# Attention by pairs of heads: fp32 values in two halves of TensorE's columns, the maxima's products tied into the order, and the modulations moved to the FFN before

## The chip, the cores and the metric

The kernel runs on one core of a Trainium2 chip. The core has TensorE (PE, matrix products into PSUM, which has eight banks of 128 partitions x 512 fp32), VectorE (DVE), ScalarE (ACT), GpSimd (POOL, which doesn't reach PSUM here) and SyncE (SP, which issues DMAs); each works off its own queue in order. The metric is the device time in microseconds; of the kernel before there are three runs.

## The reference

Two blocks run one after the other on 512 tokens of width 1024, in fp32. The first block mixes three branches (RWKV-7, S5, gated linear attention), then has a cross attention and a convolutional FFN. The second block has two layers, each with modulations of shift, scale and gate from a condition vector; layer 0 is an attention over 256 context and 512 latent tokens, layer 1 an HGRN-2. What the change touches, cut short:

```python
mod_l = silu(c) @ ada_w[i] + ada_b[i]          # 6 vectors of 1024, for latents; the same for the context
q, k = rope(rms_norm(h @ w_q)), rope(rms_norm(h @ w_k));  v = h @ w_v
# 16 heads of 64, 4 key heads: each key head serves 4 query heads
s = einsum('bkgqd,bksd->bkgqs', q, k) * 64 ** -0.5
p = softmax(s, axis=-1)
o = einsum('bkgqs,bksd->bkgqd', p, v)          # latents see all 768 keys, the context its own 256
h = h + gate * (o @ w_o)
```

## The kernel before

Values in fp32 are split into a high and a low part in the type fp32r, and a product is made of three products of parts (`Stream.multiply`, L237, and `tokens`, L250: low times high, high times low, high times high). A product whose operands are plain fp32 is one instruction in the program.

The modulations of layer 0 are made by `Products.steps` (L1483): 12 groups of 512 columns, each with four loads of 512 KB on SP's queue, eight fp32 products of 32 columns (L1494) in four column groups of TensorE (`tile_position`), a copy, and four products that turn the result (L1500). A step is half a group. Four groups are steps of `Context.steps` (L2076), which `conv_ffn` (L1328) takes in as a filler: `b.fill(m % 2)` (L1352) before each pair of feature tiles m from 2 to 21. The other eight groups are steps of `more`, taken inside the attention.

`attn_proj` (L1642) projects tokens to queries, keys and values; it runs while `ahead(0)` already prepares the first pair of heads. The accumulators of the projection are four PSUM banks (`acc2a`), the rest of the work shares four banks (`ps2a`).

`attend` (L1698) does 16 heads. For a pair g, `ahead(g)` is a generator of 13 steps: two with transposes of the queries (each followed by casts on ACT, subtractions on DVE and copies on POOL), then for each of the two heads one step with the scores against the context and four with two products of 384 columns (L1749) whose maxima DVE takes out of PSUM (L1751), and one that turns the maxima and writes their negatives by DMA as a 65th row under the queries. A head has seven units: six key tiles of 128 for the 512 latent queries, and one for the 256 context queries. `scores(h, u)` (L1762) makes two products per tile and ACT's exponential (L1773), then splits the result into `ph` and `pl` on POOL, DVE or ACT by the number of the unit. `values(h, u)` (L1785) makes three products per tile (L1792 to L1794); V has a 65th column of ones, so that a row of the sum is the softmax's denominator. `divide(g)` (L1808) brings the denominators into 12 rows by DMA, inverts them, spreads them by products (L1820) and scales the output.

The loop at L1841 writes the order down: scores of unit i, a step of `ahead` of the next pair, every seventh time a step of the modulations, values of unit i - 3. It is the order of priorities; a planner at compile time, which has times of its own for each instruction, places instructions on each engine's queue by priority and by when it expects their inputs.

Of the kernel before, what the change touches and what calls it, by code (L numbers as in the profile page):

```python
# [17 lines left out]
P = 128  # L18
# [1623 lines left out]
def attn_proj(b, st, hs, t0, tabs, p2, w, Q, K, V):  # L1642
# [5 lines left out]
    def take(i, t, acc):  # L1648
# [49 lines left out]
def attend(b, Q, K2, V, out, high, low, p2, psc, ctx, more):  # L1698
# [5 lines left out]
    Vh, Vl = V  # L1704
# [4 lines left out]
    def ahead(g):  # L1709
# [13 lines left out]
        for c0, c1 in ((0, 2), (2, 6)):  # L1723
            p = psc.tile([P, 512], F32, tag="ps", name="qt")[:, : (c1 - c0) * P]
            for t in range(c0, c1):
                nc.tensor.transpose(p[:, (t - c0) * P : (t - c0 + 1) * P],
                                    Q[kv][:, t, 2 * g % 4 : 2 * g % 4 + 2].rearrange("p h d -> p (h d)"), b.ident)
            s = slice(c0 * P, c1 * P)
            for a in range(2):
# [3 lines left out]
                if g == 0:  # L1733
                    nc.scalar.copy(q2[a][64:, s], q2[a][:64, s].bitcast(F32))
                else:
                    nc.gpsimd.tensor_scalar(q2[a][64:, s], q2[a][:64, s].bitcast(F32), 1.0, 0.0, op0=ALU.mult, op1=ALU.add)
            yield
        mx = p2.tile([P, 2, 6], F32, tag="mx", name="mx")
        m2 = p2.tile([P, 2, 4, 2], F32, tag="m2", name="m2")
        for a in range(2):  # L1740
            sc = psc.tile([P, 2, n0], F32, tag="ps", name="sc")
            for t in range(2):
                nc.tensor.matmul(sc[:, t], q2[a][:, t * P : (t + 1) * P], K2[:, kv, old], start=True, stop=True)
            nc.vector.tensor_reduce(mx[:, a, :2], sc, axis=AX.X, op=ALU.max)
            yield
            for t in range(2, 6):
                for f in range(2):
                    sc = psc.tile([P, 512], F32, tag="ps", name="sc")[:, : T // 2]
                    nc.tensor.matmul(sc, q2[a][:, t * P : (t + 1) * P], K2[:, kv, f * T // 2 : (f + 1) * T // 2],  # L1749
                                     start=True, stop=True)  # L1750
                    nc.vector.tensor_reduce(m2[:, a, t - 2, f : f + 1], sc, axis=AX.X, op=ALU.max)  # L1751
                yield
# [9 lines left out]
    def scores(h, u):  # L1762

        q2, q1 = (q[h % 2] for q in ready[h // 2][:2])
        K1 = ready[h // 2][2]
        kv = h // 4
        p = pss.tile([P, 512], F32, tag="st", name="st")
        for k, q, o in [(u, new, p)] if u < 6 else [(k, old, p[:, k * n0 : (k + 1) * n0]) for k in range(2)]:
            c = slice(k * P, (k + 1) * P)
            nc.tensor.matmul(o, K1[:, c], q1[:, q], start=True, stop=False)  # L1770
            nc.tensor.matmul(o, K2[:, kv, c], q2[:, q], start=False, stop=True)
# [3 lines left out]
        n = 7 * h + u  # L1775
        if n % 5 == 3:
            nc.scalar.copy(ph, pr)  # L1777
        else:
            (nc.vector if n % 5 == 1 else nc.gpsimd).tensor_scalar(ph, pr, 1.0, 0.0, op0=ALU.mult, op1=ALU.add)
        (nc.vector if n % 3 == 1 else nc.gpsimd).tensor_tensor(pl, pr, ph.bitcast(F32), op=ALU.subtract)  # L1780
        return ph, pl

    accs, sums, O, L = {}, {}, {}, {}

    def values(h, u, ph, pl):  # L1785
        kv = h // 4
        if u in (0, 6):
            accs[h] = psa.tile([P, 512], F32, tag="acc", name="acc")[:65, : 4 * P if u == 0 else n0]
        acc = accs[h]
        for k, x in [(u, slice(0, 512))] if u < 6 else [(k, slice(k * n0, (k + 1) * n0)) for k in range(2)]:  # L1790
            first, last = k == 0, k == (1 if u == 6 else 5)
# [5 lines left out]
        g, r = h // 2, h % 2 * 64  # L1797
        if u == 5 and h % 2 == 0:
            sums[g] = p1.tile([65, T], F32, tag="s", name="sums")
            O[g] = po.tile([P, T], F32, tag="O", name="O")  # L1800
        at = new if u == 5 else old
        nc.scalar.copy(O[g][r : r + 64, at], acc[:64])
        nc.scalar.copy(sums[g][r : r + 1, at], acc[64:])
        if u == 6 and h % 2:
            parts.append(divide(h // 2))
# [24 lines left out]
    pp = b.pool("atp", 5, ctx=ctx)  # L1830
    p4 = b.pool("at4", 4, ctx=ctx)
    pss, psa = (b.pool(f"ps2{n}", k, PSUM, ctx=ctx) for n, k in (("s", 2), ("v", 2)))
    po = b.pool("ato", 2, ctx=ctx)
    p1 = b.pool("at1", 1, ctx=ctx)
    pick = p1.tile([12, 6, P], F32, name="pick")
# [3 lines left out]
    todo = [(h, u) for h in range(16) for u in range(7)]  # L1839
    made, parts, lead, side = [], [], 3, iter(())  # L1840
    for i in range(len(todo) + lead):  # L1841
        if i < len(todo):
            h, u = todo[i]
            made.append(scores(h, u))
            if h % 2 == 0 and u == 0 and h < 14:
                side = ahead(h // 2 + 1)
        next(side, None)
        if i % 7 == 3:
            next(more, None)
        if i >= lead:  # L1850
            values(*todo[i - lead], *made[i - lead])
            made[i - lead] = None
            if i == len(todo) + lead - 1 or i % 14 == 12 and i > 14:
                next(parts.pop())
    run(more)
# [213 lines left out]
class Context:  # L2069
# [6 lines left out]
    def steps(self, wk, pool, n=256):  # L2076
        b = self.b
        cx = b.pool("cx", 1, ctx=self.c, side="right")
        with ExitStack() as c:
            self.products = Products(b, self.mod[0], cx, b.pool("cin", 1, ctx=c, side="right"))  # L2080
            ps, ada = b.pool("psad", 1, PSUM, ctx=c), b.pool("ada", 4, ctx=c, side="right")
            yield from self.products.steps(range(4), lambda: ps.tile([P, 512], F32, tag="ps", name="mods"), ada)
# [12 lines left out]
def block2(b, st, X, h, late, old_, c, out, ctx):  # L2095
# [13 lines left out]
    with ExitStack() as c0:  # L2109
# [3 lines left out]
        with ExitStack() as c1:  # L2113
            kp = b.pool("kv", 1, ctx=c1, side="right")
            K2 = kp.tile([P, 4, T], F32R, name="K2")
            V = kp.tile([P, 6, 4, C64 + 1], F32R, name="Vh"), kp.tile([P, 6, 4, C64], F32R, name="Vl")
            nc.gpsimd.memset(V[0][:, :, :, C64:].bitcast(F32), 1.0)
            K = kp.tile([P, 6, 4, C64], F32, name="K")
            at2 = b.pool("at2", 2, ctx=c1, side="right")
            ps = b.pool("ps2a", 4, PSUM, ctx=c1)  # L2120
            with ExitStack() as c2:
# [3 lines left out]
                st.banks("acc2a", 4, c2)  # L2125
# [3 lines left out]
                for n_, _ in enumerate(project(old_.h, 0, [None] * 2)):  # L2129
                    if n_ == 1:  # L2130
                        late(ps)
# [3 lines left out]
                more = old_.products.steps(range(4, 12), lambda: ps.tile([P, 512], F32, tag="ps", name="mods"), st.raw)  # L2135
                att = attend(b, Q, K2, V, o, high, low, at2, ps, c, more)
                for n_, _ in enumerate(project(h, 2, [[z[:, t] for z in tabs] for t in range(4)])):
                    if n_ == 11:
                        keys(b, K, ((0, 2), (2, 6)), K2, ps)
# [12 lines left out]
            with ExitStack() as c2:  # L2152
                st.banks("acc2b", 4, c2)
                parts, h = cut(*mods), space()
# [5 lines left out]
        ps = b.pool("ps2c", 2, PSUM, ctx=cp)  # L2160
# [94 lines left out]
```

## Time and profile before

| | us |
|---|---|
| three runs: median (lowest to highest) | 3176.72 (3175.66 to 3180.91) |
| profiled execution | 3179.53 |
| its span, first to last instruction | 3177.7 |
| mean granted TensorE clock | 0.983 of 2.4 GHz |

The span counts from the first to the last instruction of the program; busy times of an engine are unions of its instructions' times. A product's record starts when it enters the array and ends when its result is out, so successive products overlap; how long one occupies the array is read from the distance of starts.

### The profile page before, as it was taken

To read this page: it belongs to the slowest core of one execution; us is meant where nothing else is said; L and a number is where in the kernel's file an instruction comes from. 1 tells how busy PE (TensorE), PEld (TensorE's weight loads), DVE (VectorE), ACT (ScalarE), POOL (GpSimd) and SP (SyncE) were. 2 spreads that over 40 slices of the span, in tenths; PEclk is the share of its full clock that TensorE was granted. 3 is DMA by queue.
4 is the path that set the end of the run, shared out by engine and by line. 5 is a ranking of instruction groups with operands and counts; after the bars stand their busy time and mean duration, and the time that the engine had idled before them with its cause. 6 is when DMAs were issued, how large, how long until landed. Compare 5 with 4: busy or idle time off the path is not lost.

```text
span 3177.7 us, 51604 instructions
## 1 busy us (share of the span) xinstructions
PE 3069.4 (97%) x20456; PEld 2634.9 (83%) x20456; DVE 1841.9 (58%) x3374; ACT 1246.9 (39%) x2436; POOL 748.0 (24%) x827
## 2 busy tenths in 40 slices
PE   8999899989999999999999999999999999899998
PEld 6888677769797888896669988888999998788888
DVE  6545495556566555777767684333655656653445
ACT  4333233325454334645655221212544444332323
POOL 3322141220030000568765000000322223210002
PEclk9999998999999999999999999999999999999999
DMA  4122223324244332432225473121421111123333
GB/s 141 58 74 68 55 74 92 120 88 138 74 139 160 120 100 87 143 101 82 72 84 162 145 257 110 60 67 58 135 73 54 48 60 47 47 77 96 95 97 120
DMA packets 114786, 308.19 MB, mean 97 GB/s; under 512 B 32224, under 2 KB 37040, under 8 KB 114032
## 3 DMA queue, kind: packets, MB, share of 16 engines
q1 hardware_dynamic: 109904, 293.94, 29.6%
q10 hardware_dynamic: 4640, 10.95, 1.0%
q8 instruction: 161, 2.64, 0.3%
q14 instruction: 81, 0.66, 0.1%
HBM read 295.18 MB, written 8.39 MB: 96 GB/s over the span
## 4 chain that ended last, share of the span: by engine, by line
PE 88%; DVE 6%; POOL 2%; ACT 2%; issue 1%; DMA 1%; SPq 0%; DVEq 0%; POOLq 0%; ACTq 0%
PE acc L244 61%; PE ps L527 3%; PE gate L1199 3%; PE acc L265 2%; PE acc L266 2%; PE acc L267 2%; PE ps L1984 2%; DVE wl L207 1%; PE mods L1494 1%; PE ss L349 1%; PE rstd L425 1%; PE sc L1749 1%; PE st L1770 1%; PE pp L527 1%; PE acc L1792 1%
## 5 line engine op out<-in xcount | busy, mean ns | idle before, releaser
L207 DVE TENSOR_TENSOR wl<-raw,wh 128x512 fp32r<-128x512 f32 (+1 forms) x779 | 577.5, 744 | 495.9 <-ACT wh L206 492.2
L206 ACT CAST wh<-raw 128x512 fp32r<-128x512 f32 (+1 forms) x899 | 537.5, 603 | 829.8 <-PE acc L244 667.6
L244 PE MATMUL acc<-hh,wl 128*128 128x512 f32 (+1 forms) x2296 | 759.8, 363 | 9.8 <-DVE th L1222 4.2
L244 PE MATMUL acc<-hl,wh 128*128 128x512 f32 (+1 forms) x2296 | 759.0, 362 | 0.0
L244 PE MATMUL acc<-hh,wh 128*128 128x512 f32 (+1 forms) x2296 | 758.0, 361 | 0.0
L244 PEld LDWEIGHTS acc<-hh,wl 128*128 128x128 f32 x2296 | 401.7, 189 | 85.4 <-issue 5.1
L244 PEld LDWEIGHTS acc<-hh,wh 128*128 128x128 f32 x2296 | 402.7, 189 | 69.2 <-issue 1.9
L244 PEld LDWEIGHTS acc<-hl,wh 128*128 128x128 f32 x2296 | 402.6, 189 | 65.0 <-issue 0.6
L207 POOL TENSOR_TENSOR wl<-raw,wh 128x512 fp32r<-128x512 f32 (+1 forms) x120 | 142.3, 1189 | 1096.5 <-ACT wh L206 1093.3
L244 PE MATMUL acc<-mh,wl 128*128 128x512 f32 (+1 forms) x848 | 261.2, 334 | 1.2 <-DVE wl L207 0.8
L244 PE MATMUL acc<-mh,wh 128*128 128x512 f32 (+1 forms) x848 | 260.1, 331 | 0.0
L244 PE MATMUL acc<-ml,wh 128*128 128x512 f32 (+1 forms) x848 | 259.9, 331 | 0.1
L244 PEld LDWEIGHTS acc<-mh,wl 128*128 128x128 f32 x848 | 150.1, 188 | 18.4 <-DVE wl L207 1.2
L244 PEld LDWEIGHTS acc<-mh,wh 128*128 128x128 f32 x848 | 151.0, 188 | 17.0
L244 PEld LDWEIGHTS acc<-ml,wh 128*128 128x128 f32 x848 | 150.4, 188 | 17.1 <-DVE ml L343 0.3
L354 POOL TENSOR_TENSOR rs<-rs,ct_all 128x2 f32<-128x2 f32 (+1 forms) x32 | 27.7, 866 | 448.1 <-DVE rs L416 448.1
L265 PE MATMUL acc<-wl,hh 128*128 128x256 f32 x448 | 126.5, 285 | 1.5 <-DVE Xc L1560 1.5
L266 PE MATMUL acc<-wh,hl 128*128 128x256 f32 x448 | 126.6, 284 | 0.0
L267 PE MATMUL acc<-wh,hh 128*128 128x256 f32 x448 | 125.8, 284 | 0.0
L1560 DVE SCALAR_TENSOR_TENSOR X<-acc,mod,X 128x256 f32<-128x256 f32 (+1 forms) x112 | 65.2, 593 | 95.1 <-PE acc L244 94.8
L1608 ACT ACTIVATE t<-acc 128x512 f32<-128x512 f32 x66 | 34.7, 528 | 193.5 <-PE acc L244 193.5
L1780 POOL TENSOR_TENSOR pl<-pr,ph 128x512 fp32r<-128x512 f32 x75 | 103.0, 1383 | 9.0 <-ACT ph L1777 4.4
(604 smaller groups left out, 5767.9 us busy)
## 6 DMA issues: line engine op xcount, KB each, us to landing
raw<-in_ffn_in_dram SPq DMA_DIRECT2D x88, 512.0 KB, 3.5
ada<-in_ada_dram SPq DMA_DIRECT2D x48, 512.0 KB, 4.2
w<-in_ada_dram SPq DMA_DIRECT2D x48, 512.0 KB, 4.4
raw<-in_ffn_w_up_dram SPq DMA_DIRECT2D x44, 512.0 KB, 3.6
raw<-in_ffn_out_dram SPq DMA_DIRECT2D x32, 512.0 KB, 3.6
raw<-in_hg_w_dram SPq DMA_DIRECT2D x32, 512.0 KB, 3.6
raw<-in_ffn_out_dram SPq DMA_DIRECT2D x40, 384.0 KB, 3.1
raw<-in_w_gate_dram SPq DMA_DIRECT2D x24, 512.0 KB, 3.4
```

The costliest lines, as they stand in the source:

```text
L206: nc.scalar.copy(h, x)
L207: (nc.gpsimd if self.help and n else nc.vector).tensor_tensor(l, x, h.bitcast(F32), op=ALU.subtract)
L244: nc.tensor.matmul(z[0], w, z[x], start=k == 0 and n == 0, stop=k == ks - 1 and n == 2)
L265: nc.tensor.matmul(acc, xh, wl, start=k == 0, stop=False)
L266: nc.tensor.matmul(acc, xl, wh, start=False, stop=False)
L267: nc.tensor.matmul(acc, xh, wh, start=False, stop=k == ks - 1)
L527: nc.tensor.matmul(out(r, ci), lhsT(r, ci), rhs(r, ci), start=start, stop=stop)
L1199: nc.tensor.matmul(acc, w, x, start=k + i == 0, stop=k == 7 and i == 2)
L1560: return lambda i, acc: b.nc.vector.scalar_tensor_tensor(X[:, i], acc, gate[:, i : i + 1], X[:, i], op0=ALU.mult, op1=ALU.add)
L1608: nc.scalar.activation(t, a, AF.Tanh, scale=0.5)
L1780: (nc.vector if n % 3 == 1 else nc.gpsimd).tensor_tensor(pl, pr, ph.bitcast(F32), op=ALU.subtract)
L1984: nc.tensor.matmul(p[:, c], kc[:, c * P : (c + 1) * P], qc[:, c * P : (c + 1) * P], start=True, stop=True)
```

## The change

Four things change. In the FFN the filler is asked for one step more at each pair of tiles, and `Context.steps` makes all 12 groups of modulations, so the attention has none. V is kept in fp32 without parts and without the ones column. The attention goes by pairs of heads: 56 units instead of 112, each with four score products into two banks, one exponential of 1024 columns, and for each key tile two fp32 products, one per head, into the lower and the upper 64 columns of the array. The denominators are made by products with a matrix of ones of 32 columns, out of two sums of three units each (POOL adds) for the latents and out of the unit itself for the context; they come as four rows per pair, and DVE adds two and two. And each step of `ahead` hands out its last product, behind which, by `issue_after`, the values or the scores of the unit are placed on TensorE's queue. The banks are now three for `ps2c` (shared), five for the projection, then four for two pairs of score banks and one for the values. The copies of the queries move from POOL to DVE.

```diff
@@ conv_ffn
-                b.fill(m % 2)
+                b.fill(1 + m % 2)
@@ attn_proj
-            h, l = (z[:, t, :, :C64] for z in V)
-            nc.scalar.copy(h, a)
-            nc.vector.tensor_tensor(l, a, h.bitcast(F32), op=ALU.subtract)
+            nc.scalar.copy(V[:, t], a)
@@ attend, ahead
-                    nc.gpsimd.tensor_scalar(q2[a][64:, s], q2[a][:64, s].bitcast(F32), 1.0, 0.0, op0=ALU.mult, op1=ALU.add)
-            yield
+                    nc.vector.tensor_scalar(q2[a][64:, s], q2[a][:64, s].bitcast(F32), 1.0, 0.0, op0=ALU.mult, op1=ALU.add)
+            yield ins
@@ attend, scores
-        pr = p4.tile([P, 512], F32, tag="pr", name="pr")
+    def scores(g, u):
+        K1, kv = ready[g][2], g // 2
+        p = pss.tile([P, 2, 512], F32, tag="st", name="st")
+        for a in range(2):
+            q2, q1 = (q[a] for q in ready[g][:2])
+            for k, q, o in [(u, new, p[:, a])] if u < 6 else [(k, old, p[:, a, k * n0 : (k + 1) * n0]) for k in range(2)]:
+                c = slice(k * P, (k + 1) * P)
+                nc.tensor.matmul(o, K1[:, c], q1[:, q], start=True, stop=False)
+                nc.tensor.matmul(o, K2[:, kv, c], q2[:, q], start=False, stop=True)
+        pr = pp.tile([P, 2, 512], F32, tag="pr", name="pr")
         nc.scalar.activation(pr, p, AF.Exp)
-        ph, pl = (pp.tile([P, 512], F32R, tag=z, name=z) for z in ("ph", "pl"))
...
+        return pr
+    def add_up(g, at, prs):
+        acc = psc.tile([P, 512], F32, tag="ps", name="den")[:, : at.stop - at.start]
+        for n, pr in enumerate(prs):
+            c = 32 * n
+            nc.tensor.matmul(acc[c : c + 32], ones, pr, start=True, stop=True, tile_position=(0, c))
+        nc.scalar.copy(sums[g][:, at], acc)
@@ attend, values
-            nc.tensor.matmul(acc, Vh[:, k, kv], pl[:, x], start=first, stop=False)
-            nc.tensor.matmul(acc[:64], Vl[:, k, kv], ph[:, x], start=False, stop=False)
-            nc.tensor.matmul(acc, Vh[:, k, kv], ph[:, x], start=False, stop=last)
+            for a in range(2):
+                nc.tensor.matmul(acc[a * 64 : a * 64 + 64], V[:, k, kv], pr[:, a, x], start=k == 0,
+                                 stop=k == (1 if u == 6 else 5), tile_position=(0, 64 * a))
+        if u < 6:
+            if u % 3 == 0:
+                three[u // 3] = pr
+            else:
+                o = ps_.tile([P, 2, 512], F32, tag="sm", name="sm") if u % 3 == 1 else three[u // 3]
+                nc.gpsimd.tensor_tensor(o, three[u // 3], pr, op=ALU.add)
+                three[u // 3] = o
...
+        nc.scalar.copy(O[g][:, at], acc)
+        if u == 5:
+            waiting.append(lambda z=[three[n][:, a] for a in range(2) for n in range(2)]: add_up(g, new, z))
+        else:
+            add_up(g, old, [pr[:, a, k * n0 : (k + 1) * n0] for a in range(2) for k in range(2)])
@@ attend, divide
+        two = p2.tile([12, 2, P], F32, tag="s2", name="s2")
+        for a in range(2):
+            for n in range(2):
+                r = 64 * a + 32 * n
+                nc.sync.dma_start(two[6 * a : 6 * a + 6, n], sums[g][r : r + 1].rearrange("o (t q) -> o t q", q=P))
         inv = p2.tile([12, P], F32, tag="s", name="s")
-        for a in range(2):
-            nc.sync.dma_start(inv[6 * a : 6 * a + 6], sums[g][64 * a : 64 * a + 1].rearrange("o (t q) -> o t q", q=P))
+        nc.vector.tensor_tensor(inv, two[:, 0], two[:, 1], op=ALU.add)
         nc.vector.reciprocal(inv, inv)
@@ attend, the loop
-    todo = [(h, u) for h in range(16) for u in range(7)]
-    made, parts, lead, side = [], [], 3, iter(())
+    todo = [(g, u) for g in range(8) for u in range(7)]
+    made, parts, waiting, lead, side = [], [], [], 2, iter(())
+    def behind():
+        ins = next(side, None)
+        return ExitStack() if ins is None else b.tc.issue_after(ins.ins)
     for i in range(len(todo) + lead):
+        if waiting:
+            waiting.pop()()
+        with behind():
+            if i >= lead:
+                values(*todo[i - lead], made[i - lead])
+                made[i - lead] = None
+        with behind():
+            if i < len(todo):
+                g, u = todo[i]
+                made.append(scores(g, u))
+                if u == 0 and g < 7:
+                    side = ahead(g + 1)
+        if i > 8 and i % 7 == 5:
+            next(parts.pop())
+    next(parts.pop())
@@ Context.steps
-            yield from self.products.steps(range(4), ...)
+            yield from self.products.steps(range(12), ...)
@@ block2
-            ps = b.pool("ps2a", 4, PSUM, ctx=c1)
+            psc = b.pool("ps2c", 3, PSUM, ctx=c1)
-                st.banks("acc2a", 4, c2)
+                st.banks("acc2a", 5, c2)
```

## Rows read from the trace of the kernel before

**Rows 1.** The page, part 1: busy us (share of the span) xinstructions, by engine.

```profile
PE 3069.4 (97%) x20456; PEld 2634.9 (83%) x20456; DVE 1841.9 (58%) x3374; ACT 1246.9 (39%) x2436; POOL 748.0 (24%) x827
```

**Rows 2.** Windows: us, busy (x) of PE PEld DVE ACT POOL, PEclk, DMA share, GB/s.

```profile
940.00:1260.00 320.00, 320.00 (x1488) 258.21 (x1487) 181.86 (x287) 123.77 (x206) 2.71 (x4) 1.00 0.36 116
1306.00:1323.00 17.00, 10.97 (x80) 10.68 (x79) 15.90 (x35) 11.16 (x24) 9.11 (x11) 0.77 0.50 163
...
1441.00:1660.00 219.00, 212.23 (x1100) 143.75 (x1100) 162.86 (x276) 134.67 (x263) 173.24 (x180) 0.98 0.26 83
```

**Rows 3.** Groups in the attention: line, shapes, count | busy us, mean ns | idle before.

```profile
L1494 PE MATMUL mods<-ada,silu 128*32 128x512 f32 x128 | 24.9, 632 | 0.9 <-DMA ada<-in_ada_dram 0.7
L1500 PE MATMUL mods<-ct_all,mods 128*128 128x2 f32 x64 | 7.7, 241 | 0.0
...
L1773 ACT ACTIVATE pr<-st 128x512 f32<-128x512 f32 x112 | 64.9, 597 | 50.1 <-PE st L1771 43.6 <-POOL ph L1779 2.1 <-POOL pl L1780 1.5
```

**Rows 4.** Timeline of PE in the attention: start us, us, engine, line, what.

```profile
1633.15 0.39 PE L1793 MATMUL acc<-ph,Vl 128*64 128x512 f32 x1
1633.38 0.39 PE L1794 MATMUL acc<-ph,Vh 128*65 128x512 f32 x1
1633.70 1.05 PE L1494 MATMUL mods<-ada,silu 128*32 128x512 f32 x4
1634.68 0.50 PE L1770 MATMUL st<-q,K 65*128 65x512 f32 x1
1635.02 0.39 PE L1771 MATMUL st<-q,K 128*128 128x512 f32 x1
```

**Rows 5.** Timeline of PE in the convolutional FFN, around steps of the modulations.

```profile
1009.07 0.39 PE L244 MATMUL acc<-hh,wh 128*128 128x512 f32 x1
1009.39 1.92 PE L1494 MATMUL mods<-ada,silu 128*32 128x512 f32 x16
...
1011.59 0.40 PE L244 MATMUL acc<-hl,wh 128*128 128x512 f32 x1
...
1124.38 0.40 PE L244 MATMUL acc<-hh,wh 128*128 128x512 f32 x1
...
1125.74 0.39 PE L244 MATMUL acc<-hl,wh 128*128 128x512 f32 x1
```

**Rows 6.** Timeline of PE in RWKV: fp32 products of 64 rows and 64 columns.

```profile
109.88 0.68 PE L527 MATMUL ps<-Z,Y 64*64 64x64 f32 x16
110.40 0.63 PE L527 MATMUL ps<-T,No 64*64 64x64 f32 x16
```

**Rows 7.** Waits of PE and its weight loads, attention: us in total, times, longest.

```profile
PE acc L1792 <- DVE pl L1780: 1.8, 2, 1.0
...
PE acc L1792 <- POOL pl L1780: 1.3, 4, 0.7
...
PEld acc L1792 <- POOL pl L1780: 5.5, 8, 1.2
...
PEld acc L1792 <- DVE pl L1780: 3.2, 3, 1.4
PEld sc L1749 <- DVE m L1751: 2.5, 3, 0.8
```

**Rows 8.** The tile pr: engine, operation, count: ns min/median/max, first and last start.

```profile
L1780 POOL TENSOR_TENSOR pl<-pr,ph x75: 1259/1292/2330, 1448.8 to 1656.9; 128x512 fp32r<-128x512 f32 x75
...
L1780 DVE TENSOR_TENSOR pl<-pr,ph x37: 615/1086/1779, 1447.1 to 1654.3; 128x512 fp32r<-128x512 f32 x37
...
L1779 DVE TENSOR_SCALAR ph<-pr x23: 350/550/1499, 1444.1 to 1655.3; 128x512 fp32r<-128x512 f32 x23
```

**Rows 9.** Timeline at the end of the FFN and the start of the projection.

```profile
1314.31 0.41 DVE L1230 TENSOR_TENSOR X<-X,acc 128x256 f32<-128x256 f32 x1
...
1321.41 0.86 DVE L466 SCALAR_TENSOR_TENSOR X<-X,vt,rstd 128x256 f32<-128x256 f32 x2
...
1322.33 0.58 PE L265 MATMUL acc<-wl,hch 128*128 128x256 f32 x1 [4.35 <-DVE X L466]
```

More of the change, by code (lines that the diff above doesn't have):

```diff
@@ L1695, in keys, with attend @@
                 nc.vector.tensor_tensor(l, r, h.bitcast(F32), op=ALU.subtract)
-def attend(b, Q, K2, V, out, high, low, p2, psc, ctx, more):
+def attend(b, Q, K2, V, out, high, low, p2, psc, ctx):
     nc = b.nc
-    Vh, Vl = V
     T, n0 = 6 * P, 2 * P
@@ L1742, in ahead @@
             for t in range(2):
-                nc.tensor.matmul(sc[:, t], q2[a][:, t * P : (t + 1) * P], K2[:, kv, old], start=True, stop=True)
+                ins = nc.tensor.matmul(sc[:, t], q2[a][:, t * P : (t + 1) * P], K2[:, kv, old], start=True, stop=True)
             nc.vector.tensor_reduce(mx[:, a, :2], sc, axis=AX.X, op=ALU.max)
-            yield
+            yield ins
             for t in range(2, 6):
@@ L1760, in ahead @@
         yield
[L1762 to L1771, printed above, removed]
-        pr = p4.tile([P, 512], F32, tag="pr", name="pr")
-        nc.scalar.activation(pr, p, AF.Exp)
-        ph, pl = (pp.tile([P, 512], F32R, tag=z, name=z) for z in ("ph", "pl"))
[L1775 to L1781, printed above, removed]
@@ L1787, in values @@
+    accs, sums, O, L, three = {}, {}, {}, {}, {}
+    def add_up(g, at, prs):
[4 more added lines that the diff above has]
+        nc.scalar.copy(sums[g][:, at], acc)
+    def values(g, u, pr):
+        kv = g // 2
         if u in (0, 6):
-            accs[h] = psa.tile([P, 512], F32, tag="acc", name="acc")[:65, : 4 * P if u == 0 else n0]
@@ L1789, in values @@
-        acc = accs[h]
+            accs[g] = (psa.tile([P, 512], F32, tag="acc", name="acc") if u == 0 else
+                       psc.tile([P, 512], F32, tag="ps", name="acc")[:, :n0])
+        acc = accs[g]
         for k, x in [(u, slice(0, 512))] if u < 6 else [(k, slice(k * n0, (k + 1) * n0)) for k in range(2)]:
-            first, last = k == 0, k == (1 if u == 6 else 5)
-            nc.tensor.matmul(acc, Vh[:, k, kv], pl[:, x], start=first, stop=False)
-            nc.tensor.matmul(acc[:64], Vl[:, k, kv], ph[:, x], start=False, stop=False)
-            nc.tensor.matmul(acc, Vh[:, k, kv], ph[:, x], start=False, stop=last)
+            for a in range(2):
+                nc.tensor.matmul(acc[a * 64 : a * 64 + 64], V[:, k, kv], pr[:, a, x], start=k == 0,
+                                 stop=k == (1 if u == 6 else 5), tile_position=(0, 64 * a))
@@ L1795, in values @@
+        if u < 6:
[5 more added lines that the diff above has]
+                three[u // 3] = o
         if u < 5:
             return
-        g, r = h // 2, h % 2 * 64
-        if u == 5 and h % 2 == 0:
-            sums[g] = p1.tile([65, T], F32, tag="s", name="sums")
+        at = new if u == 5 else old
@@ L1800, in values @@
+        if u == 5:
+            sums[g] = p1.tile([P, T], F32, tag="s", name="sums")
             O[g] = po.tile([P, T], F32, tag="O", name="O")
[L1801 to L1805, printed above, removed]
+        nc.scalar.copy(O[g][:, at], acc)
+        if u == 5:
+            waiting.append(lambda z=[three[n][:, a] for a in range(2) for n in range(2)]: add_up(g, new, z))
+        else:
+            add_up(g, old, [pr[:, a, k * n0 : (k + 1) * n0] for a in range(2) for k in range(2)])
+            parts.append(divide(g))
@@ L1829, in attend @@
     pq = b.pool("atq", 2, ctx=ctx)
-    pp = b.pool("atp", 5, ctx=ctx)
-    p4 = b.pool("at4", 4, ctx=ctx)
-    pss, psa = (b.pool(f"ps2{n}", k, PSUM, ctx=ctx) for n, k in (("s", 2), ("v", 2)))
+    pp = b.pool("atp", 4, ctx=ctx)
+    ps_ = b.pool("ats", 3, ctx=ctx)
+    pss, psa = (b.pool(f"ps2{n}", k, PSUM, ctx=ctx) for n, k in (("s", 2), ("v", 1)))
     po = b.pool("ato", 2, ctx=ctx)
     p1 = b.pool("at1", 1, ctx=ctx)
+    ones = p1.tile([P, 32], F32, name="ones")
+    nc.gpsimd.memset(ones, 1.0)
     pick = p1.tile([12, 6, P], F32, name="pick")
@@ L1838, in attend @@
                        b.ident[:12, t : t + 7 : 6].unsqueeze(2).to_broadcast([12, 2, 64]))
-    todo = [(h, u) for h in range(16) for u in range(7)]
-    made, parts, lead, side = [], [], 3, iter(())
-    for i in range(len(todo) + lead):
[L1842 to L1855, printed above, removed]
+    todo = [(g, u) for g in range(8) for u in range(7)]
[3 more added lines that the diff above has]
+        return ExitStack() if ins is None else b.tc.issue_after(ins.ins)
+    for i in range(len(todo) + lead):
+        if waiting:
[13 more added lines that the diff above has]
+    next(parts.pop())
 def lower_bounds(b, pool):
@@ L2081, in steps @@
             ps, ada = b.pool("psad", 1, PSUM, ctx=c), b.pool("ada", 4, ctx=c, side="right")
-            yield from self.products.steps(range(4), lambda: ps.tile([P, 512], F32, tag="ps", name="mods"), ada)
+            yield from self.products.steps(range(12), lambda: ps.tile([P, 512], F32, tag="ps", name="mods"), ada)
         self.mods = [Mod(b, self.mod, 0, k) for k in range(2)]
@@ L2130, in block2 @@
                     if n_ == 1:
-                        late(ps)
+                        late(psc)
                 st.help = False
                 o = []
-                more = old_.products.steps(range(4, 12), lambda: ps.tile([P, 512], F32, tag="ps", name="mods"), st.raw)
-                att = attend(b, Q, K2, V, o, high, low, at2, ps, c, more)
+                att = attend(b, Q, K2, V, o, high, low, at2, psc, c)
                 for n_, _ in enumerate(project(h, 2, [[z[:, t] for z in tabs] for t in range(4)])):
                     if n_ == 11:
-                        keys(b, K, ((0, 2), (2, 6)), K2, ps)
+                        keys(b, K, ((0, 2), (2, 6)), K2, psc)
                     if n_ >= 11:
@@ L2153, in block2 @@
                 st.banks("acc2b", 4, c2)
+                ps = psc
                 parts, h = cut(*mods), space()
@@ L2159, in block2 @@
         st.banks("acc2c", 6, cp)
-        ps = b.pool("ps2c", 2, PSUM, ctx=cp)
+        ps = b.pool("ps2d", 2, PSUM, ctx=cp)
     with ExitStack() as c:
```

12 lines of the change are left out of this document (4 added, 8 removed).

## Prediction

> **What bounds the kernel now.** I read the page's busy shares first, then the busy times by stretch, the groups of instructions and the order of work inside the attention, and last the waits. The page [rows 1] shows TensorE busy for 97% of the span and no other engine above 58%, so a change is worth what it takes from TensorE or from the gaps between its products. Four stretches matter [rows 2]. In the convolutional FFN (940 to 1260 us) TensorE is busy all the time: whatever is put there lengthens it one for one. At 1306 to 1323 us it is busy 11.0 of 17 us, at a granted clock of 0.77. In the attention (1441 to 1660 us) it is busy 212.2 of 219 us, but "busy" counts overlapping ends there, so I go by starts of successive products.
>
> Five prices are needed. A fp32r product of 512 columns takes 0.23 us from start to start (1633.15 to 1633.38) [rows 4]. A fp32 product appears as two records, since the 64 products of the eight groups of modulations in the attention stand as 128 [rows 3]. Two fp32 products in different column groups (four records) run side by side: from L1794 at 1633.38 to L1771 at 1635.02 are 1.64 us; less two ordinary steps of 0.23 the excursion costs 1.18 us [rows 4]. The row gives all four 1.05 us, where one alone lasts 0.63 in the mean [rows 3], so they overlap. Some 0.3 us of the 1.18 is not streaming but entry and exit: L1494 starts 0.32 us after L1794 instead of 0.23, and the product after it takes 0.34 instead of 0.23. In the FFN a whole group of modulations, 16 records, takes 1011.59 - 1009.07 - 0.46 = 2.06 us, and its eight turned products 1125.74 - 1124.38 - 0.46 = 0.90 us [rows 5].
>
> **The change part by part.**
>
> *Modulations out of the attention.* Eight of twelve groups leave it: 24.9 us of L1494 and 7.7 us of L1500 [rows 3], together -32.6 us. Their 32 loads of 512 KB also leave SP's queue there, where they stood between the maxima's rows, the sums' rows and the output weights.
>
> *Modulations into the FFN.* Eight groups at 2.06 + 0.90 are 23.7 us, as long as a group runs whole. In the attention a group comes in pieces and costs 32.6 / 8 = 4.1 us. With b.fill called 30 times rather than 10, groups follow each other closely. I take 3.3 us per group, near the whole ones, +26 us, between 24 and 33. The 16.8 MB over 320 us add 52 GB/s to 116 GB/s at a DMA share of 0.36 [rows 2]; the stretch at 1306 us carries 163 GB/s at 0.50, so I charge no waiting for weights. The load of a group waits in SP's queue for its buffer and holds the weights queued behind it; three raw buffers cover that.
>
> *Values.* A unit of a pair of heads had six fp32r products, 6 x 0.23 = 1.38 us (the last unit's are twelve of half the columns). It becomes one pair of 64-column fp32 products for each key tile, side by side: one excursion of 1.18 us as above, since it is entered from a fp32r product of `ahead` and left to another. 56 x (1.18 - 1.38) = -11.2 us. That two tiles of 64 columns overlap is shown only for tiles of 64 rows as well: 16 such records take 0.52 us from 109.88 to 110.40 [rows 6], 0.033 us apiece, less than one record of 64 columns streams by itself (twice its columns, 0.053 us at 2.4 GHz). If wider weights load longer, add up to 0.05 us each; if they don't overlap, see the rivals.
>
> *Sums.* The ones-column of V was free; now each pair has four 32-column fp32 products of 512 columns (an excursion, 1.18 us) and four of 256 columns behind the values of the last unit: half of the streaming, 0.43 us, and a change of column width that no row shows, 0 to 0.35 us, of which I take 0.2. 8 x (1.18 + 0.63) = +14.5 us.
>
> *Splits of the probabilities.* The casts and subtractions on POOL, DVE and ACT go. The waits for them go too: TensorE's products idled 1.8 + 1.3 us for `pl`, its weight loads, which partly lie beside products, 5.5 + 3.2 us [rows 7]. I take the middle, -6, between -3 and -9. What is late next is the exponential: 512 columns take 0.597 us [rows 3], 1024 some 1.05 us (an estimate from that row, doubled, less a start), against two units of lead, over 5 us. So it is hidden. POOL's four adds of 1024 columns per pair cost twice 1.29 us each [rows 8], 10.3 us of a pair's 22, and are wanted only at the next unit but one. The 16 further small DMAs and the add before the reciprocal lie three units ahead of their use; at the very end the output products of the earlier heads cover them.
>
> *The tie and the banks.* Values now stand behind one step of `ahead`, scores behind the next, on TensorE's queue. A step needs two of three banks of psc (four before), which are freed by DVE's maxima. If DVE is late, the step waits, and behind it values, the next step and scores; behind these ACT's exponential. Before, DVE was busy 162.9 us [rows 2], 20.4 per pair; 37 subtractions and 23 copies at their medians [rows 8] take 6.6 per pair out, four copies of q and one add bring 2 in: 15.8 per pair. TensorE needs per pair 28 x 0.23 = 6.4 us for scores, 8.3 for values, 1.8 for sums, and by their columns at the same rate, with 0.3 us for each change of form, about 5 for `ahead` and 2 for the reciprocals' rows: 23.5 us. So DVE has room on average, but its work is lumpy: after the transposes of q it has four subtractions and four copies. The nearest row is the maxima's wait of today, 2.5 us in all [rows 7]; with a bank less I take 1 us for each of seven pairs, +7, between 0 and +25.
>
> *Banks of the projection.* At 1317 to 1322 us TensorE waits 4.35 us for DVE's last L466, which reads a bank of the norm before [rows 9]; the projection's accumulators lie there. With three banks below and five for the accumulators the first one lies a bank lower, which the last FFN product left at 1314.7 us [rows 9]. One accumulator's products can start earlier; the next may wait again. I take -3, between 0 and -7.
>
> Sum: -32.6 + 26 - 11.2 + 14.5 - 6 + 7 - 3 = -5.3 us. The profiled execution took 3179.5 us, 1.8 us around its span; this makes 3174.2. The median of the three runs lies 2.8 us lower, so I expect 3171.4 us as a median. Streaming hardly shrinks: the values' gain is eaten by the sums.
>
> **Rivals.**
>
> *DVE held by POOL (slower).* DVE's subtraction takes 0.615 us at the least, 1.086 in the median and 1.779 at most, its copy 0.350 and 1.499; the excess is about a POOL instruction's 1.29 us [rows 8]. POOL's instructions now last 2.6 us, for 10.3 of 23.5 us. Six DVE instructions of that kind per pair (four copies, two `ol`) meet one with chance 0.44 and wait 1.3 us in the mean, 3.4 us per pair, and the maxima stand behind them. It decides when this comes to more than the 1 us per pair that I allow, which it does if the copies fall in the same unit as an add; against it, no add is due in the last and the first unit of a pair, when the copies are. At 3 us per pair rather than 1: +14, 3185 us.
> The Trainium skill (SBUF — State Buffer, "Who interferes with whom") says that a DVE copy in a two-port mode or an instruction with two SBUF inputs and a GpSimd instruction block each other whole, the second waiting for the first; by that rule the longer adds hurt, and the rows' maxima agree with it. This is the mechanism of this rival.
>
> *Relief (faster).* The fixed order keeps DVE fed, the waits of +7 don't come, the projection gains 7, and groups of modulations run whole: -7 - 4 - 2: 3158 us. For it speak DVE's fall from 20.4 to 15.8 us per pair; against it the bank less.
>
> *The halves run one after the other (it doesn't do what it says).* Then each unit streams 0.86 us more: 56 x 0.86 = +48, 3220 us. The overlaps of rows 4 and 6 speak against it.
>
> *The FFN starves.* SP's queue, held by a modulation's buffer, lets the weights come late: 1 us in each of 12 groups, 3183 us. Against it, TensorE has no gap there today.
>
> **How the numbers follow.** Forecast 0.46 (its own range 3165 to 3178), DVE held 0.21, relief 0.24, halves in series 0.04, starving 0.05. The range 3150 to 3194 reaches from beyond relief to past the DVE case and leaves out the serial halves and the far end of the widest term, the waits of the tie. 0.2% is 6.4 us, about what a measurement can tell. The forecast case is faster by more than that in a third of itself, 0.16, else the same, 0.30. Relief is faster, 0.24. DVE held is slower in 0.17 and the same in 0.04; starving slower 0.04, the same 0.01; serial halves slower. Faster 0.40, same 0.35, slower 0.25.
>
> **What would show it.** The FFN stretch longer by 24 to 28 us with TensorE still without gaps. Value products of 64 columns in pairs, some 7 ns apart, 1.18 us from step to step. From the first scores to the last value some 189 us instead of 217. The gap before the first projection product shorter. In the waits, `sc` on `m` under 10 us. Wrong would be: value records spaced by a whole stream, a pair taking over 25 us with `sc` waiting for DVE, or modulations costing over 4 us a group in the FFN.

## The result and the profile after

The changed kernel takes 3208.16 us (median of 4) where the kernel before takes 3178.81 on the same chip: a ratio of 1.0087, 95% interval 1.0072 to 1.0101. It is slower by 0.9%; forecast were 3171.4 us and a range of 3150 to 3194.

The page's first part of the kernel after (busy us, share of the span, instructions), as [rows 1]:

```profile
span 3205.5 us, 51216 instructions
PE 3085.7 (96%) x20456; PEld 2608.1 (81%) x20456; DVE 1810.8 (56%) x3344; ACT 1212.3 (38%) x2326; POOL 660.2 (21%) x689
```

DVE, ACT and POOL do less than before, TensorE has the same number of records, and still the span is 27.8 us longer. I cut both profiled executions at the same products (last product of a stage, first of the next) and read the lengths from the timelines of TensorE. Every stretch in this document comes from one execution of its kernel, every median of a changed kernel from four to twelve:

| stretch | before, us | after, us | forecast | measured |
|---|---|---|---|---|
| up to the convolutional FFN | 926.1 | 928.5 | 0 | +2.4 |
| FFN, to its last product | 386.7 | 417.8 | +26 | +31.1 |
| gap before the projection | 9.5 | 9.5 | -3 | 0 |
| projection, and gap to the first scores | 119.1 | 120.9 | 0 | +1.8 |
| attention, first scores to first output product | 218.6 | 211.8 | -28.3 | -6.8 |
| output products | 78.5 | 80.0 | 0 | +1.5 |
| the rest | 1439.1 | 1436.9 | 0 | -2.2 |

So 21.5 of the 33.1 us by which the sum was wrong lie in the attention, 5.1 in the FFN, 3 in the projection's gap. The windows of the kernel after (columns as in [rows 2]) for the FFN, the projection's gap and the attention:

```profile
940.00:1260.00 320.00, 320.00 (x1545) 242.59 (x1544) 163.29 (x269) 113.93 (x193) 1.99 (x3) 1.00 0.49 159
1339.00:1356.00 17.00, 10.47 (x82) 10.18 (x82) 15.70 (x35) 11.87 (x26) 10.46 (x12) 0.80 0.51 169
1477.00:1689.00 212.00, 194.13 (x903) 104.33 (x904) 133.75 (x239) 91.64 (x140) 81.82 (x41) 0.91 0.01 4
```

The FFN has no gap (320 of 320 us), so it grew by products. The attention is idle for 17.9 of 212 us, and its granted clock is 0.91 where it was 0.98. Its waits name the engine (total us, times, longest):

```profile
PEld sc L1748 <- DVE m L1750: 28.1, 22, 2.6
PE sc L1748 <- DVE m L1750: 11.2, 6, 2.2
DVE s L1823 <- DMA s<-sums: 10.3, 6, 7.4
PE sc L1748 <- DVE q L1735: 4.2, 6, 2.7
```

TensorE waits for the maxima, once in almost each pair, and DVE itself waits for the denominators' DMA: 7.4 of its 10.3 us are one wait at the end, behind the last maximum, and the other five are 0.4 to 0.6 us each. One place where TensorE waits, first DVE, then POOL, then TensorE (start us, us, engine, line, what, [idle before]):

```profile
1563.40 1.96 DVE L1823 TENSOR_TENSOR s<-s 12x128 f32<-12x128 f32 x1 [0.64 <-DMA s<-sums]
1565.40 0.94 DVE L1824 RECIPROCAL s<-s 12x128 f32<-12x128 f32 x1
1566.27 0.48 DVE L1750 TENSOR_REDUCE m<-sc 128x1 f32<-128x384 f32 x1
1566.78 0.69 DVE L1731 TENSOR_TENSOR q<-qt,q 64x512 fp32r<-64x512 f32 x1
1567.50 0.86 DVE L1735 TENSOR_SCALAR q<-q 64x512 fp32r<-64x512 f32 x1
```

```profile
1562.84 2.38 POOL L1800 TENSOR_TENSOR sm<-pr 128x1024 f32<-128x1024 f32 x1 [9.58 <-ACT pr L1772]
1565.74 2.35 POOL L1800 TENSOR_TENSOR sm<-sm,pr 128x1024 f32<-128x1024 f32 x1 [0.52 <-ACT pr L1772]
```

```profile
1564.31 0.33 PE L1748 MATMUL sc<-K,q 128*128 128x384 f32 x1
1566.80 0.45 PE L1748 MATMUL sc<-K,q 128*128 128x384 f32 x1 [2.16 <-DVE m L1750]
1567.18 1.50 PE L1793 MATMUL acc<-pr,V 128*64 128x512 f32 x4
1568.61 1.08 PE L1748 MATMUL sc<-K,q 128*128 128x384 f32 x2
```

Read it from the end. TensorE's second product of the step needs a bank that the maximum of 1566.27 frees. That maximum stands on DVE's queue behind the reciprocal and the sum of the denominators. The sum, of 12x128 numbers, waits 0.64 us for its DMA and lasts 1.96 us, until 0.14 us after POOL's add has ended at 1565.22. What follows on TensorE is slow too: the clock, in windows around it (third column from the end):

```profile
1564.00:1566.00 2.00, 0.64 (x3) 0.22 (x2) 1.97 (x2) 1.02 (x1) 1.48 (x2) 1.00 0.00 0
1566.00:1568.00 2.00, 1.20 (x5) 0.38 (x5) 1.94 (x4) 0.00 (x0) 2.00 (x1) 0.92 0.00 0
1568.00:1570.00 2.00, 2.00 (x6) 1.19 (x5) 1.97 (x5) 0.00 (x0) 0.08 (x1) 0.50 0.00 0
1570.00:1572.00 2.00, 2.00 (x8) 1.30 (x8) 0.81 (x2) 0.57 (x1) 0.00 (x0) 0.72 0.04 8
```

After the wait of 2.16 us the granted clock goes to 0.50, the 1.2 GHz level, for some 3.4 us by these windows (they lose 0.16, 1.00 and 0.56 us of full clock, together 1.7, which is 3.4 us at half). So a wait of 2.2 us costs some 3.9 us.

### The profile page after: what moved, and what is told of

Its sections match the earlier page's. It is cut to its first block, busy times and chain, and to the rows that moved or that the text cites. A ratio compares the mean times of both kernels' runs of the same rounds, so it can differ in the third digit from the quotient of the medians.

```text
span 3205.5 us, 51216 instructions
## 1 busy us (share of the span) xinstructions
PE 3085.7 (96%) x20456; PEld 2608.1 (81%) x20456; DVE 1810.8 (56%) x3344; ACT 1212.3 (38%) x2326; POOL 660.2 (21%) x689
## 4 chain that ended last, share of the span: by engine, by line
PE 88%; DVE 6%; issue 2%; ACT 1%; DMA 1%; POOL 1%; SPq 1%; DVEq 0%; POOLq 0%; ACTq 0%
PE acc L244 60%; PE ps L527 3%; PE gate L1199 3%; PE acc L265 2%; PE acc L266 2%; PE acc L267 2%; PE ps L2005 2%; PE acc L1793 2%; DVE wl L207 1%; PE sc L1748 1%; PE mods L1494 1%; PE ss L349 1%; PE rstd L425 1%; PE st L1769 1%; PE pp L527 1%
## 5 line engine op out<-in xcount | busy, mean ns | idle before, releaser
L354 POOL TENSOR_TENSOR rs<-rs,ct_all 128x2 f32<-128x2 f32 (+1 forms) x32 | 27.5, 859 | 462.7 <-DVE rs L416 462.7
L1609 DVE SCALAR_TENSOR_TENSOR t<-t,acc 128x512 f32<-128x512 f32 x66 | 39.3, 596 | 104.3 <-ACT t L1608 104.3
```

The lines of the kernel that those rows point to most:

```text
L1609: nc.vector.scalar_tensor_tensor(t, t, 1.0, a, op0=ALU.add, op1=ALU.mult)
```

## The experiments

Theory A: the small sum and the reciprocal at the head of DVE's queue, waiting for DMA and held by POOL's add, stop the maxima, and the clock doubles the price. Theory B: the tied order with three banks stops TensorE whoever is late. Theory C: the modulations were cover for waits of the attention. Times are given by the ratio to the kernel before, run on the same chip, and by the stretches of the table.

**The modulations alone** (the kernel before with this part of the change):

```
-                b.fill(m % 2)
+                b.fill(1 + m % 2)
...
-            yield from self.products.steps(range(4), ...
+            yield from self.products.steps(range(12), ...
...
-                more = old_.products.steps(range(4, 12), ...
+                more = iter(())
```

> The kernel before, with one part of the change alone: the eight groups of modulations go from the attention into the convolutional FFN (12 groups there, a fill of one or two steps before every pair of tiles); values, sums, order and banks of the attention stay as they were. Theory A (the change loses its time on DVE's queue: the denominators' add and reciprocal stand ahead of the maxima, wait for DMA, and POOL's longer adds hold DVE): the move by itself is nearly neutral. The FFN gets 28 to 31 us longer, the attention (first scores to first output product, 218.6 us before) 28 to 33 us shorter; median 3175 to 3182 us. Theory C (the modulations were the cover of the attention's waits, and without them any form of it stalls): the FFN gets 28 to 31 us longer, but the attention only some 10 to 15 us shorter, with waits for pl or sc of over 15 us; median 3192 to 3200 us.

Measured: 3197.98 us, ratio 1.0038 (1.0024 to 1.0051). FFN 417.6 us (+30.9), attention 199.8 (-18.8). The move alone costs some 12 us. Both theories have the FFN right; the attention gives back less than theory A has (28 to 33) and more than theory C (10 to 15): 18.8 of the 32.6 us of products, so that theory C holds for the kernel before, for 13.8 us. TensorE idles for 15.5 of 200 us, where it was 6.8 of 219 [rows 2]: that is 8.7 of the 13.8, and the rest is not assigned. Its waits, against [rows 7], where `pl` stood at 1.3 and 1.8 us on TensorE:

```profile
PE acc L1792 <- POOL pl L1780: 5.7, 12, 0.8
PE st L1770 <- ACT pr L1773: 3.2, 6, 1.3
PE acc L1792 <- DVE pl L1780: 2.4, 3, 1.0
```

**POOL's adds left out**:

```
-            if u % 3 == 0:
-                three[u // 3] = pr
-            else:
...
-                nc.gpsimd.tensor_tensor(o, three[u // 3], pr, op=ALU.add)
-                three[u // 3] = o
+            three[u // 3] = fixed
```

> The changed kernel without POOL's adds of the probabilities: the sums' products read a tile of ones instead, so the kernel leaves out the adding up (32 instructions of 2.37 us); products, order and ties are the same. Theory A: DVE's small add falls from 1.96 to 0.28 us, its copies of q from 0.86 to 0.42 us, and TensorE's wait of some 2.5 us per pair in the step of the maxima becomes one of under 1 us, too short for the granted clock to fall; attention 211.7 us to some 185 to 193, median 3183 to 3191 us. Theory B (the tied order with three banks makes TensorE wait, whoever is late): the waits stay, as three banks and the order are the same; median above 3202 us. Theory C: no change either, above 3202 us.

Measured: 3188.02 us, ratio 1.0012 (1.0001 to 1.0024), attention 188.6 us. DVE's small sum (duration min/median/max in ns):

```profile
L1818 DVE TENSOR_TENSOR s<-s x7: 278/279/280, 1503.5 to 1649.9; 12x128 f32<-12x128 f32 x7
```

In the kernel after the same row reads:

```profile
L1823 DVE TENSOR_TENSOR s<-s x7: 280/1956/2259, 1508.6 to 1672.3; 12x128 f32<-12x128 f32 x7
```

TensorE's order (but for the places of the sums' products), ties and banks are the same, and 23.2 us are gone: theory B is out as the cause. Nor is the wait for the DMA the greater part: it stands here as it did, with the reciprocal and the maximum behind it:

```profile
1551.95 0.28 DVE L1818 TENSOR_TENSOR s<-s 12x128 f32<-12x128 f32 x1 [0.66 <-DMA s<-sums]
...
1553.13 0.48 DVE L1750 TENSOR_REDUCE m<-sc 128x1 f32<-128x384 f32 x1
```

From one turning of the maxima to the next, a pair takes 24.2 us here, 27.3 in the kernel after, and 23.5 in the next experiment, where the sum stands elsewhere. What POOL's adds hold costs some 3 us per pair, and the place with its DMA wait and the reciprocal some 0.7.

**The sum and the reciprocal moved behind the maxima** (complete kernel):

```
         yield
+        with b.tc.issue_after(dve[0].ins):
+            nc.vector.tensor_tensor(inv, two[:, 0], two[:, 1], op=ALU.add)
+            nc.vector.reciprocal(inv, inv)
+        yield
...
+        if i > 8 and i % 7 == 4:
+            next(parts[-1])
```

Here `dve[0]` is the last maximum written down.

> The changed kernel, complete, with one thing moved: DVE's add and reciprocal of the denominators are tied behind the eight maxima of the first head of the next pair, and no longer stand among the copies of q; POOL's adds stay. Theory A: the wait for the DMA (10.3 us in all), the held add (1.96 us each) and the reciprocal (0.94 us) leave the place where TensorE waits; only the held copy of q (0.86 instead of 0.42 us) stays. The wait per pair falls from 2.5 to under 1 us, the granted clock in the attention from 0.93 to over 0.97 in the mean; attention 185 to 193 us, median 3183 to 3191 us. If the copies held by POOL are the greater part, the wait falls only to some 1.5 us: median 3195 to 3202 us. Theory B: unchanged, above 3202 us.

Measured: 3188.41 us, ratio 1.0008 (0.9996 to 1.0021), no longer to be told from the kernel before; attention 189.3 us, with TensorE's order the same product for product. The window of the attention, and one pair's maxima with the two products of a step together again:

```profile
1476.00:1666.00 190.00, 183.39 (x905) 99.58 (x904) 122.70 (x240) 91.65 (x140) 82.50 (x41) 0.97 0.02 4
```

```profile
1558.07 0.51 PE L1748 MATMUL sc<-K,q 128*128 128x384 f32 x2
1558.51 1.08 PE L1793 MATMUL acc<-pr,V 128*64 128x512 f32 x4
```

Of the 22.5 us gained, 11.3 are idle time (17.9 less 6.6 us) and 10.7 are busy time of the same products (194.1 less 183.4), which goes with the clock: its mean in the attention rises from 0.91 to 0.97. One held instruction stays, the copy of q in the first pair (2.24 us), and with it a wait of 2.73 us.

**The tie left out** (`next(side, None)` and an empty context in `behind`):

> The changed kernel without the tie: values and scores are not bound behind the steps of the next pair, the planner places them. Theory A: DVE's queue is the same, the add waits and is held as before, and the maxima need the same banks; TensorE has at most one set of values or scores to take in the wait: median 3198 to 3210 us. Theory B: the waits of 2.5 us per pair go, attention 185 to 193 us, median 3183 to 3191 us.

Measured: 3223.98 us, ratio 1.0127 (1.0109 to 1.0144), attention 226.9 us. Outside the range of either theory: the tie is worth 15 us of the attention (0.4% by the medians). Without it the planner gathers four products of maxima at the end of a pair, and TensorE waits for all of them:

```profile
1561.32 2.02 PE L1748 MATMUL sc<-K,q 128*128 128x384 f32 x4
1565.18 0.38 PE L1754 MATMUL mt<-ct_all,mx 128*12 128x128 f32 x1 [1.84 <-DVE mx L1752]
```

**One instruction exchanged** (the sum stays in its place on DVE's queue; the planner then puts one maximum behind the next subtraction and copy of q):

```
-        nc.vector.tensor_tensor(inv, two[:, 0], two[:, 1], op=ALU.add)
+        nc.vector.tensor_reduce(inv, two.rearrange("p n q -> p q n"), axis=AX.X, op=ALU.add)
```

> The changed kernel, complete, with one instruction of DVE exchanged in its place: the two halves of the denominators are added by a reduction over one input (12x128 out of 12x256) instead of an addition with two inputs; it still waits for the DMA and the reciprocal still follows it. TensorE's order in the attention is the same. Theory A in its narrow form (a DVE instruction with two SBUF inputs is held by POOL's add for its whole length, one with a single input is not): the instruction falls from 1.96 to 0.3 to 0.5 us, the wait per pair from 2.5 to under 1.6 us, the clock falls in fewer pairs; attention 211.8 us to 188 to 197, median 3186 to 3195 us. If the wait for the DMA and the reciprocal are the cause and the hold is chance, the reduction lasts long as well or the wait stays: attention 205 to 211 us, median over 3200 us.

Measured: 3195.62 us, ratio 1.0054 (1.0035 to 1.0073), attention 197.0 us, at the upper edge of theory A's range. DVE, and POOL's add at the same time:

```profile
1569.14 0.42 DVE L1823 TENSOR_REDUCE s<-s 12x128 f32<-12x256 f32 x1 [0.65 <-DMA s<-sums]
1569.59 0.94 DVE L1824 RECIPROCAL s<-s 12x128 f32<-12x128 f32 x1
```

```profile
1568.58 2.37 POOL L1800 TENSOR_TENSOR sm<-pr 128x1024 f32<-128x1024 f32 x1 [9.60 <-ACT pr L1772]
```

The reduction runs in 0.42 us in the midst of POOL's add, where the addition took 1.96. The exchange alone is worth 14.8 of the 22.5 us by the stretch; by the medians it gives back 0.33 of the 0.79% that the late sums do, with intervals of some 0.2% on either. What stays is not the DMA and the reciprocal alone, which cost 0.7 us per pair in the run without adds: a pair takes 24.5 us here, 1.0 more than with the late sums, and TensorE waits up to 1.0 us for the subtraction that the planner put ahead of a maximum:

```profile
PE sc L1748 <- DVE q L1731: 4.5, 5, 1.0
```

The Trainium skill (SBUF — State Buffer, "Who interferes with whom") says that a DVE instruction with two SBUF inputs contends with a GpSimd instruction that reads SBUF, and a reduction never; the trace agrees (1.96 and 0.42 us). That a single input is enough to go free, as the expectation has it, is not so: a copy of q, with one input, lasted up to 2.24 us beside an add and 0.42 without.

**The copies of q on ACT**, beside the late sums (`nc.scalar.copy` in place of `nc.vector.tensor_scalar`):

> The kernel with the late sums, and besides the copies of q for pairs 1 to 7 on ACT instead of DVE. What is left of theory A there is the first pair: a copy of q held by POOL for 2.24 us, a wait of 3.3 us and the low clock behind it, and six copies of 0.63 instead of 0.42 us. Theory A: these go, attention 189.3 us to 182 to 186, median 3181 to 3186 us. Rival: ACT's copies stand ahead of exponentials, and TensorE waits for pr instead: attention 188 to 194 us, median 3187 to 3194 us.

Measured: 3182.65 us, ratio 1.0013 (0.9999 to 1.0027), attention 189.7 us: no gain that can be measured. The first pair's wait falls from 3.3 to 1.2 us between starts, but one later pair and the tail lose as much to spells of low clock, which neither expectation had (see the last section). The rival's reason shows too: TensorE waits 3.6 us for `pr`, seven times, where it was 0.9.

**Whole groups of modulations**, beside the late sums (`b.pool("ada", 6, ...)` in place of 4):

> The kernel with the late sums, and besides six instead of four buffers for the modulations' weights in the FFN, so that the planner puts eleven of twelve groups in one piece (five of twelve with four buffers). If a cut group costs 1.07 + 1.93 us instead of 1.94, the FFN falls from 417.5 us to 410 to 412 and the median to 3180 to 3184 us. If the cut costs nothing and the groups are dear for another reason (weights, the clock), the FFN stays at 416 to 418 us and the median at 3187 to 3190 us.

Measured: 3179.54 us, ratio 0.9998 (0.9987 to 1.0010). FFN 410.0 us, 7.5 less (six groups that are no longer cut make 6 x (1.07 + 1.93 - 1.94) = 6.4); attention 192.1, 2.8 more, with two more spells of low clock. A cut group and a whole one, both in the FFN of the kernel after:

```profile
1012.40 1.91 PE L1494 MATMUL mods<-ada,silu 128*32 128x512 f32 x12
1014.24 0.50 PE L244 MATMUL acc<-hl,wh 128*128 128x512 f32 x1
1014.58 0.39 PE L244 MATMUL acc<-hh,wh 128*128 128x512 f32 x1
1014.90 1.05 PE L1494 MATMUL mods<-ada,silu 128*32 128x512 f32 x4
1015.89 0.50 PE L244 MATMUL acc<-hh,wl 128*128 128x512 f32 x1
...
1109.64 0.39 PE L244 MATMUL acc<-hh,wh 128*128 128x512 f32 x1
1109.95 1.92 PE L1494 MATMUL mods<-ada,silu 128*32 128x512 f32 x16
1111.81 0.50 PE L244 MATMUL acc<-hh,wl 128*128 128x512 f32 x1
```

**All three, and the sum by a reduction:**

> The late sums, the sum by a reduction, the copies of q on ACT and six buffers for the modulations' weights together. If the causes are independent: FFN 410 to 412 us, attention 182 to 186, median 3174 to 3181 us on a chip where the kernel before takes 3178 to 3184, that is a ratio of 0.997 to 0.999. If the waits only move (ACT late, or weights late), 3183 to 3190 us and a ratio of 1.000 or more.

Measured: 3176.50 us, ratio 0.9986 (0.9975 to 0.9998), FFN 410.3, attention 186.2 us. It is faster than both kernels, by 0.14% than the one before and by about 1% than the one after.

**More casts on ACT**, in the kernel with only the modulations moved (`n % 5 in (0, 3)` in place of `n % 5 == 3`):

> The kernel with only the modulations moved, and besides 22 of POOL's 67 casts of the probabilities (0.62 us each) on ACT. That kernel's attention is 199.8 us where the loss of 32.6 us of products from 218.6 would make 186; POOL is busy 178 of 201 us there. If POOL is what bounds it (the modulations lay beside POOL's splits and were partly free), taking 13.7 us from POOL shortens the attention to 191 to 196 us and the median by 4 to 9 us against the kernel with only the modulations moved, to 3189 to 3194 us. If the attention without modulations is held by something else (maxima, banks, the clock), it stays at 198 to 202 us and the median at 3196 to 3200 us.

Measured: 3193.82 us, ratio 1.0038 (1.0020 to 1.0055), attention 199.1 us. POOL went from 178 to 162 us and nothing was gained; TensorE's waits for `pl` fell and those for ACT's `pr` rose:

```profile
PE st L1770 <- ACT pr L1773: 4.9, 7, 1.3
PE acc L1792 <- DVE pl L1780: 3.0, 4, 1.5
PE acc L1792 <- POOL pl L1780: 1.8, 5, 0.7
```

So POOL alone did not bound that form; which link of exponential, cast and subtraction does stays open.

**The modulations back in the attention**, in the version with all mends (the steps of `more` at units 3 and 5 of a pair, the fills in the FFN as before):

> The kernel with all three mends, but the eight groups of modulations back in the attention, in a bank that they share with the maxima. FFN 386 to 388 us instead of 410. If nothing in the mended attention is left to cover them, they cost there what their products cost, two pieces of 1.07 + 1.93 us and 0.8 us turned, 30 us: attention 214 to 218 us, median 3180 to 3186 us. If they still lie beside waits, as in the kernel before, they cost under 20 us: attention 200 to 206 us, median 3168 to 3174 us. If the bank that they take starves the maxima: attention over 222 us, median over 3187 us.

Measured: 3186.38 us, ratio 1.0013 (1.0002 to 1.0024). FFN 387.7 us (22.6 less), attention 213.7 (27.5 more). TensorE is idle for 5.9 of 214 us, where the version with all mends is idle for 5.5 of 186: the 27.5 us are products and not waits for the shared bank. In the new form the modulations have almost no cover left in the attention, and the move into the FFN gains some 5 us by the stretches (0.27% by the medians) as long as groups are whole. Theory C holds for the old form alone.

## Why the prediction was wrong

**The step that failed** is the cost of nothing for the denominators' sum: "the 16 further small DMAs and the add before the reciprocal lie three units ahead of their use". Its use is three units ahead, but its place on DVE's queue is among the maxima that TensorE needs at once. There it lasts 1.96 us, held by POOL's add, where it takes 0.28 without one; TensorE waits 2.16 us behind it and then runs at 1.2 GHz for 3.4 us, and a pair takes 27.3 us instead of 23.5. The wait for the DMA and the reciprocal, which stand in the same place, are some 0.7 of these 3.8 us. I asked who waits for the result and not who stands behind the instruction. With that goes "+7, between 0 and +25" for tie and banks: the late sums alone give back 22.5 us, 3.2 per pair of seven, where I had taken 1.

**Rival "DVE held by POOL"** had the mechanism and nearly the price (3 us per pair; a pair is 3.1 us shorter without the adds), but not the place: it counted copies and `ol`, not the sum, and its argument against itself ("no add is due in the last and the first unit") is wrong: POOL's add of 2.37 us begins as soon as the second exponential is there, and the last copies of q are just then on DVE (0.86 instead of 0.42 us). It also had no term for the clock, which is about half of the loss. "Relief" was right that DVE has room (busy 133.8 of 212 us), and room was not the point.

**Modulations out, -32.6 us.** In the kernel before they lay in part beside waits: taken out alone they gave 18.8. With the splits gone they count nearly in full (27.5 us to put them back). The term was right only together with the values' new form.

**Modulations in, +26.** The stretch grew by 31.1 us. Summed as the forecast did it (to the second product behind a piece, less two steps of 0.23), the eight more groups cost 30.6 us, 3.8 each and not 3.3, as seven of twelve groups are cut; with six buffers, where one is cut, they cost 23.6 us, 3.0 each. So the price of a whole group was right, and that most would run whole was not. 0.5 us of the stretch I could not assign. TensorE had no gap, so weights did not starve it.

**Values and sums.** Value products overlap, as forecast: a unit stands for 1.01 us to the next start and lengthens the step before it and the one behind it by some 0.1 each, so 1.20 where 1.18 was forecast. Where the planner puts two units together they take 2.17, and the last unit of a pair, which the sums follow, less; in the mean some 1.15: 56 x (1.15 - 1.38) = -13 us, forecast -11.2. The sums in the kernel after:

```profile
1555.68 1.06 PE L1782 MATMUL den<-sm,ones 128*32 128x512 f32 x8
1556.68 0.44 PE L1725 MATMUL qt<-ct_all,Q 128*128 128x128 f32 x2
1557.05 1.08 PE L1793 MATMUL acc<-pr,V 128*64 128x256 f32 x8
1558.06 0.64 PE L1782 MATMUL den<-pr,ones 128*32 128x256 f32 x8
1558.63 0.50 PE L1769 MATMUL st<-q,K 65*128 65x512 f32 x1
```

1.00 + 0.57 us per pair, +12.6 instead of +14.5. With the late sums a pair takes 23.5 us, which is what was worked out (23.5); that the two agree to the tenth is luck, as values and sums came out some 0.5 us lower and the rest as much higher. The halves do not run in series, and the planner kept to the tie.

**Splits, -6.** Their waits went with them and cannot be read apart; the exponential is hidden, as forecast (TensorE waits 0.9 us for `pr` in all).

**Banks of the projection, -3.** Nothing: the first product still waits for the last L466, now 4.86 us ([rows 9] 4.35). That the accumulators lie a bank lower did not free an earlier one.

**Small ones** that I had at nothing: +1.8 us before the first scores, +1.5 in the output products, and +2.4 and -2.2 ahead of and behind it all, which the change does not touch.

**What would have shown it wrong** was named: "a pair taking over 25 us with `sc` waiting for DVE", and this is what the trace shows.

## What to carry to other kernels

Cost an instruction by what stands behind it on its engine, not by who needs its result: a small step that can be held goes behind the work that another engine needs at once, here by a tie. Beside POOL's adds of 2.37 us a DVE addition with two SBUF inputs lasted 1.96 us instead of 0.28, and copies up to 2.24 instead of 0.42; a reduction over one input did the same sum in 0.42. Filler that is moved away takes its cover with it, so price it by taking it out alone, and give a filler's loads enough buffers that its groups stay whole.

## What was not expected of the hardware

The granted clock fell to the lower level after waits of TensorE of only 2.16 us, and it stayed there for some 3.4 us. And it fell without any wait: in the version with all mends, right behind the twelve products of 12 rows that spread the reciprocals, with TensorE busy throughout:

```profile
1526.00:1528.00 2.00, 2.00 (x14) 1.35 (x14) 1.36 (x3) 1.22 (x3) 1.53 (x2) 0.88 0.00 0
1528.00:1530.00 2.00, 2.00 (x6) 0.65 (x8) 1.97 (x4) 0.29 (x1) 1.09 (x1) 0.50 0.00 0
1530.00:1532.00 2.00, 2.00 (x9) 0.75 (x6) 0.26 (x1) 0.59 (x1) 0.00 (x0) 0.76 0.00 0
```

Such a spell makes a pair 25.0 instead of 23.4 us; there are two in this attention and in the one with the late sums none without a wait ahead of it. Why some pairs have one and others with the same products do not was not found.
